# A hybrid recurrent decoder step on one core: weight matrices of the first two feed-forward multiplies begun earlier

## The chip, the core and the metric

The kernel runs on one core of one Trainium2 chip. The metric is the device time of one execution in microseconds (us), the median of several runs; less is better. The engines are called PE (matrix multiply), DVE (vector), ACT (activations), POOL (GpSimd) and SP (the queue that issues the DMA transfers).

## What is computed

One layer over 1032 tokens (1024 of a new sequence and 8 single ones), 1024 wide. The part that the change touches lies between the output projection and the SwiGLU feed-forward:

```python
merged = jnp.concatenate([rmsnorm(lru_out, p['g_lru_out']), rmsnorm(s5_out, p['g_s5_out'])], axis=-1)
x32 = x.astype(F32) + g1 * (merged @ p['w_out'].astype(F32))
hn2 = rmsnorm(x32, p['norm2_g']) * (1.0 + sc2) + sh2
ffn = (jax.nn.silu(hn2 @ p['ffn_w_gate'].astype(F32)) * (hn2 @ p['ffn_w_up'].astype(F32))) @ p['ffn_w_down'].astype(F32)
```

## The kernel before

Every fp32 product is made of three PE products of split operands: a number is held as a high and a low part (`wh`, `wl` of a weight matrix, two planes of a data block), and the kernel multiplies high by high, high by low and low by high. The tokens lie in four quarters of 258; two of them make a half, called z=0 and z=1.

The gate and up multiplies use a recursive scheme with seven products in place of eight (`PRODUCTS`): X A, Z A, X S, Y S, X T, Y T and X D. The first letter is the PSUM bank in which the product gathers, the second the weight matrix: A is loaded as it is, S and T are made of sums and differences of the two loaded pieces, and D is a quarter of the second piece. One product for one half is 12 matmuls of 128x258. `gu_weights(n)` begins matrix n (even numbers are gate matrices, named g0, g1, ...; odd ones up matrices, u0, u1, ...): it issues two loads (`wf_g`, `wf_u`; there are two buffers for all of them), four sums on POOL (`sa`, `sb`) and the split of D. The splits of A, S and T are made when `get` is first called: an ACT copy for the high part and a DVE subtraction for the low one. `roomy` puts T's parts into a big pool of 24 buffers instead of the pool of two for `wh` and `wl`. With `lazy`, which only u0 has, D is split when it is first asked for.

The data of a half become ready in a chain. The output projection adds its units to `xz` on DVE, ACT squares the rows (`sqx`), PE sums the squares over the rows (`pc_n2a` for z=0, `pc_n2b` for z=1), ACT and DVE make the reciprocal root of it, PE spreads it over the partitions (`pb_n`), ACT copies it out (`rb`), and `norm2_steps` multiplies `xz` by it on DVE, scales and shifts on ACT, and splits the result into blocks `b` on ACT and DVE, some of their differences (`vn`) on POOL. The blocks are ready in four groups: B11, B21 (`b1_d_0` for z=1 and each d), T1 and T2 (`b1_d_1`), T3 and T4 (`b1_d_2`).

The stretch between the projection and the regular loop is here called the entry. There g0 and u0 are run for one half at a time, because z=1 isn't ready yet: gate z=0, up z=0, up z=1, then gate z=1 with the gate matrix loaded a second time (g0b). From matrix g1 on both halves are multiplied together. In the entry the order of the instructions of ACT, DVE and POOL is that of the code (`entry` opens a context that says so); PE's order is that of the code throughout, and a scheduler sets SP's. `multiply` runs the functions in `hooks` behind the `after` of a product; `after` copies banks out and hands results to the taker (silu for the gate). The hooks of gate z=0 begin u0 (`u_make`), split g0's S and T, and run the chain above for z=1 (`rstd_b`, `spread_b`, `norm_rest`).

Of the kernel before, what the change touches and what calls it, by code (L numbers as in the profile page):

```python
# [19 lines left out]
T = 1024  # L20
# [34 lines left out]
def body(ctx, tc, a, o):  # L55
    nc = tc.nc
    V, S, G, PE = nc.vector, nc.scalar, nc.gpsimd, nc.tensor
# [13 lines left out]
    def mul(out, x, y, e=None):  # L71
        tt(out, x, y, ALU.mult, e)

    def add(out, x, y, e=None):
        tt(out, x, y, ALU.add, e)

    def sub(out, x, y, e=None):
        tt(out, x, y, ALU.subtract, e)
# [10 lines left out]
    def f(name, w=TX, dt=F32):  # L89
        return fp.tile([P, w], dt, tag="F", name=name, padded_shape=[P, TX])  # L90

    def small(name):
        return psm.tile([P, 512], F32, tag="sm", name=name)

    def split(hi, lo, src, e=None):
        S.activation(hi, src, AF.Copy)
        tt(lo, src, hi.bitcast(F32), ALU.subtract, e)
# [26 lines left out]
    def load_raw(src, name, n=1024):  # L124
        wf = wp.tile([P, n], F32, tag="wf", bufs=2, name=f"wf_{name}")
        nc.sync.dma_start(out=wf, in_=src)
        return wf

    def split_w(wf, name, n=1024, pool=None, tags=("wh", "wl"), e=None):
        q = pool or wp  # L130
        wh = q.tile([P, n], F32R, tag=tags[0], name=f"wh_{name}")
        wl = q.tile([P, n], F32R, tag=tags[1], name=f"wl_{name}")
        split(wh, wl, wf, e)
        return wh, wl
# [14 lines left out]
    def wcols(pair, k):  # L149
        return tuple(t[:, k * P:(k + 1) * P] for t in pair)  # L150

    def acc_bank(name, w=CW):
        return pm.tile([P, 512], F32, tag="mm", name=name)[:, 0:w]
# [529 lines left out]
    after = ExitStack()  # L683
# [389 lines left out]
    for j in range(4, 20):  # L1073
        i = int(R0 + R1 * (j - 4))
# [153 lines left out]
    def four(t):  # L1228
        return t[:, 0:4 * CH].rearrange("p (b n) -> p b n", b=4)
# [6 lines left out]
    def x_load(z):  # L1236
        for d in range(4):
            xz[z].append(four(f(f"xz{z}_{d}", TT)))
            for i in range(2):
                nc.sync.dma_start(out=xz[z][d][:, 2 * i:2 * i + 2], in_=zview(a["xp"][2 * d + i], z))  # L1240
# [119 lines left out]
    def quarter(name):  # L1360
        return chunk(name, CH)
# [105 lines left out]
    TOGETHER = [(i, z) for i in range(7) for z in range(2)]  # L1467
    APART = [(i, z) for z in range(2) for i in range(7)]

    def weights_of(r0, r1, n, name, roomy=False, lazy=False):  # L1470

        sa, sb = (f(f"s{i}_{name}", 2 * n) for i in "ab")
        add(sa[:, 0:n], r1[:, 0:n], r1[:, n:2 * n], G)
        sub(sa[:, n:2 * n], sa[:, 0:n], r0[:, 0:n], G)
        sub(sb[:, 0:n], r0[:, 0:n], r1[:, 0:n], G)
        sub(sb[:, n:2 * n], r0[:, n:2 * n], sa[:, n:2 * n], G)
        src = {"A": r0, "S": sa, "T": sb}
        made = {}

        def make_d():  # L1480
            d = f(f"{name}D", 2 * n, F32R)
            made["D"] = d[:, 0:n], d[:, n:2 * n]
            split(*made["D"], r1[:, n:2 * n])

        if not lazy:
            make_d()

        def get(which, i):
            if which == "D" and lazy and "D" not in made:
                make_d()  # L1490
            if which not in made:
                kw = dict(pool=fp, tags=("F", "F")) if roomy and which == "T" else {}
                made[which] = split_w(src[which], f"{name}{which}", 2 * n, **kw)
            return tuple(t[:, i * n:(i + 1) * n] for t in made[which])

        return get

    def multiply(get, nk, xin, after, order=TOGETHER, hooks={}):

        banks = [{}, {}]  # L1500
        for i, z in order:
            bank, which, half, block = PRODUCTS[i]
            w = get(which, half)
            first = bank not in banks[z]
            if first:
                banks[z][bank] = (small(f"{bank}{z}") if bank == "Z" else acc_bank(f"{bank}{z}", 512))[:, 0:CH]
            b = banks[z][bank]
            for k in range(nk):
                (wh, wl), (xh, xl) = wcols(w, k), xin(z, k)[block]
                PE.matmul(b, lhsT=wh, rhs=xh, start=first and k == 0, stop=False, skip_group_check=True)  # L1510
                PE.matmul(b, lhsT=wh, rhs=xl, start=False, stop=False, skip_group_check=True)  # L1511
                PE.matmul(b, lhsT=wl, rhs=xh, start=False, stop=k == nk - 1, skip_group_check=True)  # L1512
            after(i, z, banks[z])
            for fn in hooks.get((i, z), ()):
                fn()


    NP = NFF // 2

    def gu_weights(n, again=""):  # L1520
        p_, j = divmod(n, 2)
        name = f"{'gu'[j]}{p_}{again}"
        r = [load_raw(a["w_gu"][2 * p_ + i, j], f"{name}_{i}") for i in range(2)]
        return weights_of(*r, 512, name, n in (1, 2 * NP - 1), n == 1)

    def dn_weights(n):

# [24 lines left out]
    def gate_up(u, get, take, **kw):  # L1552
        keep = [{}, {}]

        def after(i, z, b):
            k = keep[z]

            def copy(name, bank):
                k[name] = quarter(f"{name}{z}")
                S.activation(k[name], b[bank], AF.Copy)  # L1560

            if i == 0:
                copy("p1", "X")
            elif i == 1:
                add(k["p1"], b["Z"], k["p1"])
                take(z, 0, k["p1"])
            elif i == 2:
                copy("u2", "X")
            elif i == 3:
                copy("p5", "Y")  # L1570
            elif i == 4:
                copy("u3", "X")
                add(k["u3"], k["u3"], k["p5"], G)
                take(z, 3, k["u3"])
            elif i == 5:
                add(k["u2"], b["Y"], k["u2"])
                take(z, 1, k["u2"])
            else:
                take(z, 2, b["X"])

        multiply(get, 4, lambda z, k: blks[z][k], after, **kw)

    def gate(u):
        return lambda z, at_, src: S.activation(u[z][:, at_], src, AF.Silu)

    def up(u):
        return lambda z, at_, src: mul(u[z][:, at_], src, u[z][:, at_])


    u_first = [four(f(f"u0_{z}", TT)) for z in range(2)]  # L1590
# [11 lines left out]
    for z in range(2):  # L1602
        if z:
            x_load(1)
        for i, (m, c) in enumerate(ordered_units[z]):
            if z or i >= AHEAD:
                half_part(m, c, 0)
            half_part(m, c, 1)
            if z and i == 12:
                g_w = gu_weights(0)  # L1610
                g_w("A", 0)
            if z and i == 14:
                entry.enter_context(tc.manual_schedule(engines={ENG.Activation, ENG.DVE, ENG.Pool}))
            out_add(ubank[m, c], m, c)
            if i % 2:
                out_done(z, i // 2, m)
            if z and i == 0:
                ra = rstd_half(0, "n2a")
            if z and i == 2:
                for _ in norm2_steps(0, spread_half(0, ra)):  # L1620
                    pass

    ONE = [[(i, z) for i in range(7)] for z in range(2)]
# [8 lines left out]
    def go(n):  # L1632
        return lambda: pump(norm_b[1:], n)

    u_w = []

    def u_make():
        u_w.append(gu_weights(1))

    def u_part(which):  # L1640
        return lambda: u_w[0](which, 0)

    def norm_rest():
        entry.close()
        u_part("A")()
        u_part("T")()
        pump(norm_b[1:], 99)

    gate_up(u_first, g_w, gate(u_first), order=ONE[0],
            hooks={(0, 0): [rstd_b, u_make, lambda: g_w("S", 0)], (1, 0): [lambda: g_w("T", 0)],  # L1650
                   (2, 0): [spread_b], (3, 0): [norm_rest]})
    gate_up(u_first, u_w[0], up(u_first), order=ONE[0])
    g_w = gu_weights(0, "b")
    gate_up(u_first, u_w[0], up_first, order=ONE[1])
    gate_up(u_first, g_w, gate_second, order=ONE[1])
    nxt = gu_weights(2)
    kept = []
    for p_ in range(NP):
        if p_ == 0:
            u = u_first  # L1660
        else:
            u = [four(f(f"u{p_}_{z}", TT)) for z in range(2)]
            for j in range(2):
                n = 2 * p_ + j
                get, nxt = nxt, gu_weights(n + 1) if n < 2 * NP - 1 else None
# [62 lines left out]
    for g in range(NG):  # L1728
        nx_blocks = down_blocks(g + 1) if g < NG - 1 else None
        for q in range(4):  # L1730
            n = 4 * g + q
            get, nxt = nxt, dn_weights(n + 1) if n < 4 * NG - 1 else None

            def after(i, z, b):
                row, j, bank = TO[i]
                dst = acc[2 * q + row][:, (z + 2 * j) * CH:(z + 2 * j + 1) * CH]
                add(dst, b[bank], dst)
# [49 lines left out]
    for c, (s, n) in enumerate(LAST):  # L1787
        cc = slice(s, s + n)
        ssc = f(f"ssf{c}", n)
        for m in range(DK):  # L1790
# [13 lines left out]
            if c > 0 and m == SF:  # L1804
                r = rstd_sums(sums, D, f"nf_{c - 1}", LAST[c - 1][1], 2, f)
# [107 lines left out]
```

## Time and profile before

| | us |
|---|---|
| median of 3 runs | 1178.22 (1175.53 to 1181.87) |
| the profiled execution | 1181.37 |
| its span in the profile | 1179.2 |
| PE busy in the span | 1093.7 (93%) |
| DVE busy | 838.2 (71%) |
| ACT busy | 500.9 (42%) |
| POOL busy | 454.7 (39%) |

The profile is of one execution. Its span is what the profiler saw of the core; the time of the same execution is 2.2 us longer. Positions in the span are given as microseconds from its start. The entry lies between about 454 and 523 us.

### The profile page before, as it was taken

What the parts mean: (1) busy time and instruction counts of PE and PEld (TensorE: products, weight loads), DVE (VectorE), ACT (ScalarE), POOL (GpSimd) and SP (SyncE); (2) the same over time, 40 slices, a digit from 0 to 9 for tenths busy, and PEclk for the clock granted to TensorE, in tenths of its full rate; (3) what the DMA queues carried; (4) which work ended last, traced back from release to release, by engine and by line L of the source; (5) the groups of instructions that cost most, each with busy time, mean ns of one, the idle gap of its engine ahead of it and who ended that gap; (6) DMA issues with size and microseconds to landing.
All of it is one profiled execution on the core that took longest, in us unless ns stands there. A gap on an engine that the chain in (4) does not pass through costs nothing.

```text
span 1179.2 us, 21432 instructions
## 1 busy us (share of the span) xinstructions
PE 1093.7 (93%) x8480; PEld 1045.6 (89%) x8480; DVE 838.2 (71%) x1360; ACT 500.9 (42%) x948; POOL 454.7 (39%) x475
## 2 busy tenths in 40 slices
PE   7887888999987999589999999999999999999995
PEld 5776777897967999589999999999999999999995
DVE  6879799854977287765776677677645367778966
ACT  4433323328664155553554454454444531221254
POOL 3396535301030003464654666465532133243022
PEclk8898989899998999799999999999999999999997
DMA  9557445432043302042532443244312967459212
GB/s 339 183 157 214 149 161 156 145 99 73 19 146 108 127 37 81 30 164 100 191 154 93 160 179 145 90 180 180 117 64 75 356 271 289 161 216 298 81 50 95
DMA packets 90627, 174.92 MB, mean 148 GB/s; under 512 B 18720, under 2 KB 54304, under 8 KB 90528
## 3 DMA queue, kind: packets, MB, share of 16 engines
q1 hardware_dynamic: 90528, 173.57, 42.7%
q8 instruction: 66, 1.08, 0.4%
q14 instruction: 33, 0.27, 0.1%
HBM read 126.56 MB, written 46.98 MB: 147 GB/s over the span
## 4 chain that ended last, share of the span: by engine, by line
PE 66%; DVE 10%; ACT 4%; DMA 2%; issue 2%; POOL 1%; DVEq 0%; ACTq 0%; POOLq 0%; SPq 0%
PE X L1510 9%; PE X L1512 9%; PE X L1511 9%; PE Y L1510 4%; PE Y L1512 4%; PE Y L1511 4%; PE o L1309 3%; PE o L1308 3%; PE o L1310 3%; PE Z L1510 2%; PE Z L1511 2%; PE Z L1512 2%; DMA wf_d<-w_dn 1%; DVE acc L69 1%; PE in L144 1%
## 5 line engine op out<-in xcount | busy, mean ns | idle before, releaser
L69 POOL TENSOR_TENSOR u<-u,p 128x258 f32<-128x258 f32 x44 | 40.0, 909 | 130.2 <-ACT u L1560 120.8
L142 PE MATMUL in<-hnh,wh_in 128*128 128x344 f32 (+1 forms) x240 | 82.9, 345 | 0.0
L143 PE MATMUL in<-hnl,wh_in 128*128 128x344 f32 (+1 forms) x240 | 80.1, 334 | 0.0
L144 PE MATMUL in<-hnh,wl_in 128*128 128x344 f32 (+1 forms) x240 | 80.1, 334 | 0.0
L69 POOL TENSOR_TENSOR st_d<-wf_d 128x256 f32<-128x256 f32 x32 | 27.7, 887 | 110.9 <-PE X L1512 37.9
L69 POOL TENSOR_TENSOR sa_g<-wf_g 128x512 f32<-128x512 f32 x11 | 14.2, 1295 | 117.9 <-DVE xz L69 90.4
L69 DVE TENSOR_TENSOR acc<-X,acc 128x258 f32<-128x258 f32 x128 | 49.9, 420 | 10.3 <-PE X L1512 10.1
L142 PEld LDWEIGHTS in<-hnh,wh_in 128*128 128x128 f32 x240 | 48.2, 201 | 2.9 <-issue 2.9
L69 DVE TENSOR_TENSOR hs<-v,hs 128x516 fp32r<-128x516 f32 x32 | 46.3, 1463 | 2.6 <-ACT hs L1380 2.6
L143 PEld LDWEIGHTS in<-hnl,wh_in 128*128 128x128 f32 x240 | 47.9, 200 | 0.0
L144 PEld LDWEIGHTS in<-hnh,wl_in 128*128 128x128 f32 x240 | 47.7, 199 | 0.0
L1560 ACT ACTIVATE u<-X 128x258 f32<-128x258 f32 x88 | 33.1, 381 | 33.8 <-PE X L1512 33.8
L1309 PE MATMUL o<-ls,wh_s 128*128 128x258 f32 x128 | 37.5, 293 | 5.7 <-DVE ls L69 5.7
L87 DVE SCALAR_TENSOR_TENSOR xz<-o,mod,xz 128x258 f32<-128x258 f32 (+1 forms) x32 | 15.2, 481 | 31.4 <-PE o L1310 27.6
L1310 PE MATMUL o<-hs,wl_s 128*128 128x258 f32 x128 | 37.4, 292 | 0.0
L1308 PE MATMUL o<-hs,wh_s 128*128 128x258 f32 x128 | 37.4, 292 | 0.0
L69 POOL TENSOR_TENSOR acc<-acc,rbf 128x388 f32<-128x388 f32 x10 | 11.9, 1218 | 64.7 <-ACT rbf L201 52.9
L1308 PE MATMUL o<-hl,wh_l 128*128 128x258 f32 x128 | 36.6, 286 | 0.0
L1309 PE MATMUL o<-ll,wh_l 128*128 128x258 f32 x128 | 36.5, 285 | 0.0
L1310 PE MATMUL o<-hl,wl_l 128*128 128x258 f32 x128 | 36.1, 282 | 0.0
L69 DVE TENSOR_TENSOR u<-Y,u 128x258 f32<-128x258 f32 x44 | 18.7, 425 | 22.2 <-PE Y L1512 22.1
L69 POOL TENSOR_TENSOR v<-u 128x516 f32<-128x516 f32 x16 | 20.7, 1293 | 34.9 <-DVE u L69 34.9
(1656 smaller groups left out, 4832.2 us busy)
## 6 DMA issues: line engine op xcount, KB each, us to landing
ht<-hs SPq DMA_DIRECT2D x48, 516.0 KB, 3.0
db<-ht SPq DMA_DIRECT2D x48, 516.0 KB, 8.6
ad<-ada SPq DMA_DIRECT2D x48, 512.0 KB, 6.4
wf_g<-w_gu SPq DMA_DIRECT2D x22, 512.0 KB, 3.6
wf_u<-w_gu SPq DMA_DIRECT2D x22, 512.0 KB, 3.4
wf_d<-w_dn SPq DMA_DIRECT2D x16, 512.0 KB, 4.5
wf_in<-w_in SPq DMA_DIRECT2D x10, 512.0 KB, 4.4
x<-xt SPq DMA_DIRECT2D x8, 516.0 KB, 8.0
```

The lines of the kernel that those rows point to most:

```text
L69: (e or V).tensor_tensor(out=out, in0=x, in1=y, op=op)
L87: V.scalar_tensor_tensor(out=out, in0=x, scalar=s, in1=y, op0=op0, op1=op1)
L142: PE.matmul(ps, lhsT=wh, rhs=xh, start=first, stop=False)
L143: PE.matmul(ps, lhsT=wh, rhs=xl, start=False, stop=False)
L144: PE.matmul(ps, lhsT=wl, rhs=xh, start=False, stop=last)
L1308: PE.matmul(b, lhsT=wh, rhs=xh, start=half == 0 and k == 0, stop=False)
L1309: PE.matmul(b, lhsT=wh, rhs=xl, start=False, stop=False)
L1310: PE.matmul(b, lhsT=wl, rhs=xh, start=False, stop=half == 1 and k == 3)
L1510: PE.matmul(b, lhsT=wh, rhs=xh, start=first and k == 0, stop=False, skip_group_check=True)
L1511: PE.matmul(b, lhsT=wh, rhs=xl, start=False, stop=False, skip_group_check=True)
L1512: PE.matmul(b, lhsT=wl, rhs=xh, start=False, stop=k == nk - 1, skip_group_check=True)
L1560: S.activation(k[name], b[bank], AF.Copy)
```

## The change

The gate matrix g0 is begun four units of the projection sooner (unit 8 of z=1 in place of 12), its S and T are split inside the projection (unit 12) and no more in hooks of gate z=0. The up matrix u0 is begun inside the projection (unit 14) and no more in the first hook, its T is split there, and its D is split at once instead of lazily. g0 gets the roomy place for T as well. The spread of the reciprocal root for z=1 is put between the matmuls of product 1 of gate z=0 and the `after` of that product, by a new kind of hook (`pre`), in place of the hook of product 2. A and S of u0 are split in the hooks of products 1 and 2.

```diff
-    def multiply(get, nk, xin, after, order=TOGETHER, hooks={}):
+    def multiply(get, nk, xin, after, order=TOGETHER, hooks={}, pre={}):
...
+            for fn in pre.get((i, z), ()):
+                fn()
             after(i, z, banks[z])
...
-        return weights_of(*r, 512, name, n in (1, 2 * NP - 1), n == 1)
+        return weights_of(*r, 512, name, n in (0, 1, 2 * NP - 1))
...
-            if z and i == 12:
+            if z and i == 8:
                 g_w = gu_weights(0)
                 g_w("A", 0)
+            if z and i == 12:
+                g_w("S", 0)
+                g_w("T", 0)
             if z and i == 14:
+                u_w = gu_weights(1)
+                u_w("T", 0)
                 entry.enter_context(tc.manual_schedule(engines={ENG.Activation, ENG.DVE, ENG.Pool}))
...
-    u_w = []
-
-    def u_make():
-        u_w.append(gu_weights(1))
-
-    def u_part(which):
-        return lambda: u_w[0](which, 0)
+    def part(get, which):
+        return lambda: get(which, 0)
 
     def norm_rest():
         entry.close()
-        u_part("A")()
-        u_part("T")()
         pump(norm_b[1:], 99)
 
     gate_up(u_first, g_w, gate(u_first), order=ONE[0],
-            hooks={(0, 0): [rstd_b, u_make, lambda: g_w("S", 0)], (1, 0): [lambda: g_w("T", 0)],
-                   (2, 0): [spread_b], (3, 0): [norm_rest]})
-    gate_up(u_first, u_w[0], up(u_first), order=ONE[0])
+            pre={(1, 0): [spread_b]},
+            hooks={(0, 0): [rstd_b], (1, 0): [part(u_w, "A")], (2, 0): [part(u_w, "S")], (3, 0): [norm_rest]})
+    gate_up(u_first, u_w, up(u_first), order=ONE[0])
     g_w = gu_weights(0, "b")
-    gate_up(u_first, u_w[0], up_first, order=ONE[1])
+    gate_up(u_first, u_w, up_first, order=ONE[1])
```

The order of the instructions is set by the code and the scheduler together, so three places of it are shown, before and after.

On ACT, from the split of g0's D to the two copies `rb` of the spread, the order before is this (`sqx_2` are the squares of the last rows of z=1, `p_4700` and `u_4767` copies of banks, `u_0` the silu):

```order
L96 ACTIVATE g0D<-wf_g_1_4581 128x512
L1322 ACTIVATE sqx_2_4626<-xz_2_4099 128x516 x2
L1560 ACTIVATE p_4700<-X_4687 128x258
L1400 ACTIVATE pc_n2b<-pc_n2b,epst 128x129
L96 ACTIVATE wh_g0S<-sa_g_4583 128x1024
L1584 ACT_TABLE_LOAD
L1584 ACTIVATE u_0_3738<-p_4700 128x258
L96 ACTIVATE wh_g0T<-sb_g_4584 128x1024
L96 ACTIVATE wh_u0T<-sb_u_4727 128x1024
L1560 ACTIVATE u_4767<-X_4687 128x258
L1413 ACTIVATE rb_0_4772<-pb_n_4769 128x258
L1413 ACTIVATE rb_1_4777<-pb_n_4774 128x258
```

And after the change the same stretch of ACT is this:

```order
L96 ACTIVATE g0D<-wf_g_1_4467 128x512
L1325 ACTIVATE sqx_1_4567<-xz_1_4096 128x1032
L96 ACTIVATE wh_g0S<-sa_g_4469 128x1024
L96 ACTIVATE wh_g0T<-sb_g_4470 128x1024
L1322 ACTIVATE sqx_2_4634<-xz_2_4099 128x516
L96 ACTIVATE u0D<-wf_u_1_4663 128x512
L1322 ACTIVATE sqx_2_4634<-xz_2_4099 128x516
L1562 ACTIVATE p_4725<-X_4712 128x258
L1400 ACTIVATE pc_n2b<-pc_n2b,epst 128x129
L96 ACTIVATE wh_u0T<-sb_u_4666 128x1024
L1413 ACTIVATE rb_0_4763<-pb_n_4760 128x258
L1413 ACTIVATE rb_1_4768<-pb_n_4765 128x258
```

The splits of g0's S and T and of u0's D have moved ahead of the last squares; the `rb` copies now stand ahead of the table load and the silu, but still behind `wh_u0T`, which reads the POOL sum `sb_u`.

On DVE, around the last rows of `xz` of z=1 and the first multiply by `rb`, the order before is this:

```order
L87 SCALAR_TENSOR_TENSOR xz_2_4099<-o_1_4628,mod,xz_2_4099 128x258
L87 SCALAR_TENSOR_TENSOR xz_2_4099<-o_3_4656,mod,xz_2_4099 128x250
L69 TENSOR_TENSOR go_3_4682<-o_3_4656,mod 128x8
L69 TENSOR_TENSOR xz_2_4099<-go_3_4682,xz_2_4099 128x8
L1402 RECIPROCAL r_n2b<-pc_n2b 128x129
L69 TENSOR_TENSOR wl_g0S<-sa_g_4583,wh_g0S 128x1024
L69 TENSOR_TENSOR p_4700<-Z_4736,p_4700 128x258
L69 TENSOR_TENSOR wl_g0T<-sb_g_4584,wh_g0T 128x1024
L69 TENSOR_TENSOR wl_u0T<-sb_u_4727,wh_u0T 128x1024
L69 TENSOR_TENSOR xz_0_4093<-xz_0_4093,rb_0_4772 128x2x258
```

And after the change the same place on DVE is this:

```order
L87 SCALAR_TENSOR_TENSOR xz_2_4099<-o_1_4636,mod,xz_2_4099 128x258
L69 TENSOR_TENSOR u0D<-wf_u_1_4663,u0D 128x512
L87 SCALAR_TENSOR_TENSOR xz_2_4099<-o_3_4681,mod,xz_2_4099 128x250
L69 TENSOR_TENSOR go_3_4707<-o_3_4681,mod 128x8
L69 TENSOR_TENSOR xz_2_4099<-go_3_4707,xz_2_4099 128x8
L1402 RECIPROCAL r_n2b<-pc_n2b 128x129
L69 TENSOR_TENSOR p_4725<-Z_4747,p_4725 128x258
L69 TENSOR_TENSOR wl_u0T<-sb_u_4666,wh_u0T 128x1024
L69 TENSOR_TENSOR xz_0_4093<-xz_0_4093,rb_0_4763 128x2x258
```

The low part of u0's D, which came behind all blocks of z=1, now stands ahead of the last rows of `xz`; the low parts of g0's S and T are gone from between the reciprocal and the first multiply.

On SP, the queue of loads around u0 and g0b, as a difference (`xd` writes finished rows of `xz` back to memory):

```order
 L1331 DMA xd_0_3476<-xz_0_4093 128x1032
 L1331 DMA xd_1_3477<-xz_1_4096 128x1032
-L126 DMA wf_u_0_4722<-w_gu 128x1024
-L126 DMA wf_u_1_4724<-w_gu 128x1024
+L126 DMA wf_u_0_4661<-w_gu 128x1024
+L126 DMA wf_u_1_4663<-w_gu 128x1024
+L126 DMA wf_g0b_5041<-w_gu 128x1024
 L1331 DMA xd_2_3478<-xz_2_4099 128x1032
-L126 DMA wf_g0b_5041<-w_gu 128x1024
 L126 DMA wf_g0b_5043<-w_gu 128x1024
```

The loads themselves keep their order; only the first load of g0b has passed one write. Its buffer is that of u0's second piece, which is free once u0's D and the POOL sums have been made.

## Rows read from the trace of the kernel before

**Rows 1.** By stretch: us; busy PE, PEld, DVE, ACT, POOL; PEclk; DMA share, GB/s

```profile
454.00:523.00 69.00, 50.39 (x378) 48.05 (x377) 48.82 (x73) 39.22 (x74) 32.25 (x25) 0.85 0.24 77
...
600.00:900.00 300.00, 300.00 (x2506) 300.00 (x2505) 210.28 (x233) 143.03 (x289) 166.91 (x125) 1.00 0.37 134
```

**Rows 2.** PE's waits from 400 to 523: total, times, longest

```profile
PE X L1510 <- ACT u0D L96: 7.8, 1, 7.8
PE Y L1510 <- ACT p L1560: 5.1, 2, 3.4
PE X L1512 <- DVE u0D L69: 3.0, 1, 3.0
PE X L1512 <- DVE wl_g0S L69: 1.7, 1, 1.7
PE X L1512 <- DVE wl_g0bT L69: 0.5, 1, 0.5
```

**Rows 3.** PE's longest wait behind the entry, from 523 on

```profile
PE pc_nf L181 <- DVE ssf L69: 3.6, 2, 2.4
```

**Rows 4.** PE in the entry: start, duration, instruction, idle time before it

```profile
457.94 0.36 PE L1510 MATMUL X<-b,wh_g0S 128*128 128x258 f32 x1
...
462.30 1.76 PE L1410 MATMUL pb_n<-r_n2b,ident 128*128 128x129 f32 x8
463.81 0.37 PE L1510 MATMUL Y<-b,wh_g0S 128*128 128x258 f32 x1
...
489.40 0.58 PE L1510 MATMUL X<-b,u0D 128*128 128x258 f32 x1 [7.82 <-ACT u0D L96]
...
498.03 0.28 PE L1510 MATMUL Z<-b,wh_u0A 128*128 128x258 f32 x1
...
518.43 0.58 PE L1510 MATMUL Y<-b,wh_g0bT 128*128 128x258 f32 x1 [3.44 <-ACT p L1560]
...
522.89 0.28 PE L1510 MATMUL X<-b,wh_g1A 128*128 128x258 f32 x1
```

**Rows 5.** A stretch behind the longest wait, columns as in rows 1

```profile
494.00:498.00 4.00, 4.00 (x21) 4.00 (x20) 1.32 (x2) 0.63 (x1) 1.49 (x2) 0.51 0.39 131
```

**Rows 6.** DVE around and in the entry

```profile
438.73 0.42 DVE L69 TENSOR_TENSOR vn<-xz,vn 128x258 f32<-128x258 f32 x1
...
440.15 1.32 DVE L69 TENSOR_TENSOR vn<-xz,vn 128x258 f32<-128x258 f32 x1
...
448.13 1.22 DVE L69 TENSOR_TENSOR sqx<-sqx,sqx 128x1032 f32<-128x1032 f32 x1
...
454.07 0.48 DVE L87 SCALAR_TENSOR_TENSOR xz<-o,mod,xz 128x250 f32<-128x250 f32 x1 [2.39 <-PE o L1310]
...
465.47 2.51 DVE L69 TENSOR_TENSOR xz<-xz,rb 128x516 f32<-128x516 f32 x4
...
487.90 1.89 DVE L69 TENSOR_TENSOR b<-vn,b 128x516 fp32r<-128x516 f32 x3
...
492.48 0.68 DVE L69 TENSOR_TENSOR u0D<-wf_u,u0D 128x512 fp32r<-128x512 f32 x1
```

**Rows 7.** ACT: the split of u0's T and the copies of the spread

```profile
463.06 1.04 ACT L96 ACTIVATE wh_u0T<-sb_u 128x1024 fp32r<-128x1024 f32 x1
...
464.28 0.65 ACT L1413 ACTIVATE rb<-pb_n 128x258 f32<-128x258 f32 x2
```

**Rows 8.** POOL: a sum of g0, and the first and last of u0's four sums

```profile
439.89 1.30 POOL L69 TENSOR_TENSOR sa_g<-wf_g 128x512 f32<-128x512 f32 x1 [90.36 <-DVE xz L69]
...
455.11 1.28 POOL L69 TENSOR_TENSOR sa_u<-wf_u 128x512 f32<-128x512 f32 x1 [8.47 <-DMA wf_u<-w_gu]
...
458.95 2.27 POOL L69 TENSOR_TENSOR sb_u<-wf_u,sa_u 128x512 f32<-128x512 f32 x1
```

**Rows 9.** SP's issue of u0's two loads

```profile
450.01 0.81 SPq L126 DMA_DIRECT2D wf_u<-w_gu  x2
```

**Rows 10.** The load with the longest median landing among the page's DMA issues

```profile
db<-ht SPq DMA_DIRECT2D x48, 516.0 KB, 8.6
```

## The prediction, made before the change was run

> **What bounds the kernel now.** I read the busy times by stretch first, then PE's waits, then the places of the waits on PE's timeline, and last the engines that PE waits for. In the regular loop PE is the bound: 300.00 of 300 us busy, 2506 matmuls, so 0.12 us for one and 12 x 0.12 = 1.44 us for a product of one half [rows 1]. In the entry it is not: 50.39 of 69.00 us busy, at a mean clock of 0.85 [rows 1]. PE's waits there name whom it waits for: ACT and DVE with u0's D (7.8 and 3.0 us), ACT with a bank copy (5.1 us, two times), DVE with the low part of g0's S (1.7) and of g0b's T (0.5) [rows 2]. Behind the entry no wait is above 3.6 us, and that one is the final norm's [rows 3]. So a change of the entry is worth what it takes from the entry, provided that nothing that it delays stands in the loop.
>
> DVE is the entry's second load: 48.82 us busy of 69 [rows 1]. Its longest chain runs from the first multiply by `rb` at 465.47 to the end of the third group of blocks (T1, T2 of z=1) at 487.90 + 1.89 = 489.79, 24.3 us [rows 6]. When PE's own waits go, this chain is what PE meets next; the whole forecast turns on it.
>
> **What the change removes.** (a) g0's S is split inside the projection, so PE doesn't wait for it. From its first matmul at 457.94 to the first of the next product at 463.81 there are 5.87 us [rows 4]. The product is worth 1.44; the spread `pb_n` in between took 1.51, of which a lower clock may have made half, so it is worth 0.75 to 1.51. Lost: 2.9 to 3.7 us; I take 3.6, as PE had just stood still. (b) u0's D is split early: waits of 7.8 and 3.0 us [rows 2]. PE then runs at a granted clock of 0.51, the lower of its two levels (1.2 GHz) [rows 5]: from 489.40 to 498.03 it has two products' work, 8.63 - 3.0 - 2 x 1.44 = 2.75 us over [rows 4]. Together 13.6. (c) The first of the two waits for a bank copy, 5.1 - 3.4 = 1.7 [rows 2]: its copy stands behind scalings on ACT, and some of those stay ahead of it. I expect it to stay in kind. (d) The waits for g0b's T and for the copy in front of its last products, 0.5 + 3.4 [rows 2], and the clock behind: from 518.43 to 522.89 are 4.46 us for two products of 1.44, 1.6 over [rows 4]. Together 5.5. Gross, (a) to (d): 24.4 us. That would be the gain if nothing were late next.
>
> **What is late next.** First the start of DVE's chain. u0's loads were issued at 450.01 [rows 9], as soon as DVE's g0D had been made, which now stands ahead of an add of 1.22 us and a row update of about 0.48 (their durations in [rows 6]): 1.6 sooner, 448.4. The load landed when POOL began to sum, 455.11 - 450.01 = 5.1 later [rows 8, 9]: now 453.5. The four sums took 455.11 to 458.95 + 2.27 = 461.2, 6.1 us [rows 8]: now to 459.6. `wh_u0T` (1.04) on ACT waits for the last one, and the two `rb` copies (0.65 for the pair) stand behind it [rows 7]. So `rb` comes at about 461, whatever the spread does: the earlier place of the spread on PE is not what sets it. On DVE `wl_u0T` stands ahead of the multiply (1.2 us, by the add of 1.22 with two inputs of about the same size [rows 6]): 459.6 + 1.04 + 1.22 = 461.9. The chain begins 3.6 us sooner than at 465.47. Below, if the sums run at 1.28 each [rows 8], it is a further 1.0; I leave that out.
>
> u0D on DVE (0.68 [rows 6]) now stands ahead of the last rows of `xz`. Load at 453.5, about 0.6 for ACT's half-size copy (by 1.04 for the full size [rows 7]) and 0.68: those rows start at 454.8, where they started at 454.07 [rows 6]. PE's row sums and the spread are 0.7 late, which the wait of `rb` for POOL's sums covers: squares, row sums, root, reciprocal and spread have until 460.6. That cover goes if the landing is late, and then sums and rows are late together.
>
> With the chain's own 24.3 us the third group ends at 486.2. Everything in the chain (the low parts of u0's A and S, the differences, the splits) is still in it. What is new in it is POOL. g0b's second load stood behind u0's D on DVE, which was made at 492.48 [rows 6], when the blocks were done; so its four sums came when DVE had little to do. Now that load waits only for u0's A, and the four sums run beside DVE's last groups of blocks. What that costs is seen where g0's sums ran beside the first half's norm: a difference of 128x258 took 1.32 us at 440.15, beside a POOL sum that began at 439.89 and took 1.30 [rows 6, 8], and 0.42 at 438.73 without one [rows 6]. So one sum can cost DVE 0.9 us, and up to 1.3 if the instruction waits for the whole of it: four cost 0 (they find gaps) to 5.2. I take 4.4, nearer the upper end, because DVE's splits there follow one another without a gap (three in the row at 487.90). The third group ends at 490.6; bounds 486.2 and 491.4.
>
> This agrees with a rule of the Trainium skill, "SBUF — State Buffer", section "Who interferes with whom", which speaks against this change: a DVE instruction with two inputs in SBUF and a GpSimd instruction that reads SBUF exclude each other on a shared port, and the later one fully blocks. By the rule the four sums cost about their upper bound; if it did not hold here they would cost nothing. The row at 440.15 agrees with it: 1.32 us in place of 0.42.
>
> PE, without waits, gets to the third group's product early. From about 459.3 (row sums at 456, 1.0 for them, product Z, the spread) it has five products of gate z=0, seven of up z=0 and two of up z=1: 14 x 1.44 = 20.2, and the 1.6 of (c): 481, and some 482 by the matmuls that need this group's last block. So it waits 4 to 9 us there, mostly for DVE's blocks, some of it a product earlier. From the end of the group PE has 0.36 (three matmuls) and eleven products, 15.8, to the first product of g1: 490.6 + 16.2 = 506.8. To that I add the lower clock behind the wait, 1.5 (between 0 and the 2.75 of (b)), and 2.0 for what remains of (d): its copy isn't queued behind the same transfer any more, but other copies still are; bounds 0 and 5.5. Sum: 510.3, where it was 522.89. **The gain is 12.6 us.** Ends: 486.2 + 16.2 = 502.4, a gain of 20.5; and 491.4 + 16.2 + 2.75 + 5.5 = 515.9, a gain of 7.0.
>
> Behind the entry the order of all engines is the same, and g1's loads come with PE's products of g0b, so I put nothing there.
>
> The profiled execution took 1181.37 us (its span 1179.2, and 2.2 around it): 1181.4 - 12.6 = 1168.8. The median of the runs is 1178.22, 3.15 less, so 1165.6: I predict 1166.
>
> **Rivals.** *The sums cost nothing.* For it: sums and blocks may interleave, and some of DVE's instructions there read PSUM. Against it: 440.15. Then 502.4 and 0 to 2 of the tail: a gain of 18.5 to 20.5, so 1158 to 1160. *DVE and POOL take nearly all.* The sums hit the chain in full, the wait for the copy (d) stays, and the splits of g0b come late too, since DVE makes them behind the blocks: the 7.0 shrinks by a wait of the size of the present one for the copy, 3.4, to 3.6; 1171 to 1176. Against it: g0b's second load no longer waits for the end of the blocks, so its splits have slack. *Slower.* u0D's load is late. DVE stands still in front of the last rows of `xz`, and row sums, root, `rb` and all of z=1 with them; POOL's sums are as late. Each us of landing behind 453.5 takes a us from the gain; at 466 it is gone, and it decides for slower by over 0.5% from about 472. The page's longest median landing is 8.6 us [rows 10], 3.5 more than assumed: 1169. So only an outlier does this; the time would be above 1184. *It doesn't do what it says.* The spread is ahead of the silu, but `rb` still waits for `wh_u0T`; that is in the sum. Should `wl_g0S` or u0D yet be waited for, 3.6 or up to 13.6 return, and the time is 1169 to 1178.
>
> **Chances.** Forecast with colliding sums 0.62; sums free 0.20; nearly all taken 0.10; not what it says 0.05; slower 0.03. The range takes the bounds (1158 to 1171) and most of the third case: 1158.5 to 1174. A measurement of this kernel can tell about 0.5%, 5.9 us, from no change, so faster means below 1172.3: all of the first two cases and a part of the others, 0.85; same 0.11; slower 0.04.
>
> **What would show it.** Right: PE has no wait for `wl_g0S` and none for u0D; the first multiply by `rb` starts near 462; PE's longest wait in the entry is 4 to 9 us, for DVE's blocks `b` of z=1, in up z=1; POOL's g0b sums lie at 480 to 490, and DVE's splits of `vn` beside them last over a us; g1's first product at about 510. Wrong: PE's row sums `pc_n2b` after 458 (the load was late); DVE's splits at their usual length beside the sums (a gain near 20); a wait for `p` or for g0b's parts of over 4 us in gate z=1; waits in the loop behind g1.

## The result: 1.26% faster, and the profile after

The changed kernel takes 1164.73 us (median of 4 runs, 1164.02 to 1168.10); the kernel before, on the same chip, 1178.39. The ratio is 0.9874, 95% interval 0.9855 to 0.9893. The forecast was 1166, range 1158.5 to 1174. The profiled execution took 1164.80 us, its span is 1162.8.

First PE's waits from 400 to 523 in the changed kernel (total, times, longest; compare [rows 2]):

```profile
PE X L1511 <- DVE b L69: 3.1, 3, 1.1
PE X L1510 <- ACT u L1562: 2.8, 4, 1.3
PE pc_n2b L1396 <- ACT sqx L1322: 1.3, 1, 1.3
PE X L1510 <- ACT p L1562: 0.4, 1, 0.4
```

No wait for u0's D is left, none for g0's S and none for g0b's T. The largest sum is for DVE's blocks `b`, as forecast, in three pieces of 1.0 to 1.1 us. By stretch, with the columns of [rows 1]:

```profile
454.00:509.00 55.00, 47.25 (x377) 44.69 (x377) 48.06 (x68) 35.10 (x69) 32.68 (x25) 0.94 0.20 63
...
490.00:494.00 4.00, 4.00 (x18) 4.00 (x19) 4.00 (x8) 1.64 (x3) 0.00 (x0) 0.50 0.02 4
...
509.00:586.00 77.00, 77.00 (x645) 77.00 (x644) 54.48 (x60) 37.43 (x79) 44.28 (x34) 1.00 0.46 162
```

PE and POOL have as many instructions in the entry as in [rows 1], give or take one; ACT and DVE have five fewer each, among them the splits of g0's S and T. The entry is 55 us long instead of 69: what went is mostly standing still. DVE is now busy for 48.06 of 55.00 us. Behind the wait for the blocks PE is granted 0.50, its lower level of 1.2 GHz, for some us; behind the entry there is no gap. PE's timeline at the places of [rows 4] (start, duration, instruction, idle time before it):

```profile
453.95 0.28 PE L1510 MATMUL X<-b,wh_g0A 128*128 128x258 f32 x1
...
457.68 0.43 PE L1396 MATMUL pc_n2b<-sqx,ones 128*32 128x129 f32 x8 [1.34 <-ACT sqx L1322]
459.58 1.39 PE L1410 MATMUL pb_n<-r_n2b,ident 128*128 128x129 f32 x8
...
484.41 0.39 PE L1510 MATMUL X<-b,wh_u0S 128*128 128x258 f32 x1 [0.43 <-ACT p L1562]
...
490.00 0.58 PE L1511 MATMUL X<-b,wh_u0S 128*128 128x258 f32 x1 [1.02 <-DVE b L69]
...
490.60 0.42 PE L1510 MATMUL Y<-b,wh_u0S 128*128 128x258 f32 x1
...
493.18 0.42 PE L1510 MATMUL X<-b,wh_u0T 128*128 128x258 f32 x1
...
509.05 0.28 PE L1510 MATMUL X<-b,wh_g1A 128*128 128x258 f32 x1
```

g1's first product starts at 509.05, where it was 522.89 [rows 4]: 13.8 us sooner. The medians differ by 13.7, so the entry accounts for the gain. The two profiled executions differ by 16.6; the rest of that lies behind the entry, 1.5 us of it in the down multiply.

DVE's chain (compare [rows 6]):

```profile
454.58 1.22 DVE L69 TENSOR_TENSOR u0D<-wf_u,u0D 128x512 fp32r<-128x512 f32 x1 [1.00 <-ACT u0D L96]
...
460.65 1.23 DVE L69 TENSOR_TENSOR wl_u0T<-sb_u,wh_u0T 128x1024 fp32r<-128x1024 f32 x1 [0.45 <-ACT wh_u0T L96]
461.80 3.72 DVE L69 TENSOR_TENSOR xz<-xz,rb 128x516 f32<-128x516 f32 x6
...
482.76 3.48 DVE L69 TENSOR_TENSOR b<-vn,b 128x516 fp32r<-128x516 f32 x2
...
486.50 1.43 DVE L69 TENSOR_TENSOR b<-vn,b 128x516 fp32r<-128x516 f32 x1
...
487.85 1.50 DVE L69 TENSOR_TENSOR u<-u,u 128x258 f32<-128x258 f32 x1
```

and POOL's sums for g0b, beside the last three of these rows:

```profile
482.63 1.35 POOL L69 TENSOR_TENSOR sa_g0b<-wf_g0b 128x512 f32<-128x512 f32 x1 [2.31 <-DVE b L69]
483.95 1.74 POOL L69 TENSOR_TENSOR sb_g0b<-wf_g0b,wf_g0b 128x512 f32<-128x512 f32 x1
...
487.45 1.61 POOL L69 TENSOR_TENSOR sb_g0b<-wf_g0b,sa_g0b 128x512 f32<-128x512 f32 x1
```

The first multiply by `rb` starts at 461.80 (465.47 before [rows 6]). Three splits of `vn` in a row took 1.89 us before [rows 6]; now two take 3.48, and a product of 128x258, 0.41 before, takes 1.50. PE's last wait for the third group ends at 490.00.

The landing of g0b's load is not what set the start of these sums: its second load was issued at 466.73 and took at most 4.0 us. The sums stand behind POOL's own differences `vn` and an addition, which end at 480.3, and then wait 2.31 us for a block of DVE.

### The profile page after: what moved, and what is told of

It is laid out like the page before. It is cut to its first block, busy times and chain, and to the rows that moved or that the text cites. A ratio compares the mean times of both kernels' runs of the same rounds, so it can differ in the third digit from the quotient of the medians.

```text
span 1162.8 us, 21429 instructions
## 1 busy us (share of the span) xinstructions
PE 1088.8 (94%) x8480; PEld 1042.0 (90%) x8480; DVE 843.9 (73%) x1360; ACT 499.8 (43%) x948; POOL 456.3 (39%) x475
## 4 chain that ended last, share of the span: by engine, by line
PE 70%; DVE 17%; ACT 5%; issue 4%; POOL 2%; DMA 1%; SPq 0%; DVEq 0%; ACTq 0%; POOLq 0%
PE X L1510 9%; PE X L1511 9%; PE X L1512 9%; PE Y L1510 5%; PE Y L1511 5%; PE Y L1512 5%; PE o L1308 2%; PE o L1309 2%; PE o L1310 2%; PE Z L1511 2%; PE Z L1512 2%; PE Z L1510 2%; DVE rw L69 1%; PE in L142 1%; PE in L143 1%
## 5 line engine op out<-in xcount | busy, mean ns | idle before, releaser
L69 DVE TENSOR_TENSOR acc<-Y,acc 128x258 f32<-128x258 f32 x64 | 26.7, 424 | 10.4 <-PE Y L1512 9.5
```

Source lines behind the costliest of these rows:

```text
L69: (e or V).tensor_tensor(out=out, in0=x, in1=y, op=op)
```

## The experiments

Theory: the waits for u0's D were the largest loss, and what is left is set by DVE's chain of blocks, from the first multiply by `rb` to the third group, stretched by POOL's sums. Main rivals: the early start of both matrices makes the gain by itself; every wait of PE counts by itself; POOL's sums cost nothing; the spread ahead of the silu is the heart of it.

The table gives for each kernel the ratio of its time to the kernel before on the same chip, and from its trace three times counted from PE's first matmul of g0: the first multiply by `rb` on DVE (chain), PE's first matmul of Y S in up z=1, for which X S must be done (Y S), and PE's first matmul of g1 (entry). The kernel before took 1180 to 1181 us there (median), so ratios are compared and not times.

| kernel | ratio (95%) | chain | Y S | entry |
|---|---|---|---|---|
| before | 1 | 11.60 | 47.05 | 69.02 |
| changed | 0.9874 (0.9855 to 0.9893) | 7.85 | 36.65 | 55.10 |
| changed, again | 0.9874 (0.9858 to 0.9890) | 7.88 | 36.66 | 55.09 |
| u0's D lazy again | 0.9924 (0.9906 to 0.9942) | 7.23 | 42.75 | 61.11 |
| before with u0's D at once | 0.9968 (0.9954 to 0.9982) | 12.15 | 41.37 | 63.11 |
| g0 late again | 0.9918 (0.9897 to 0.9940) | 9.45 | 43.08 | 60.24 |
| spread late again | 0.9872 (0.9853 to 0.9890) | 10.50 | 37.51 | 55.39 |
| g0's sums kept | 0.9835 (0.9814 to 0.9856) | 7.95 | 32.49 | 51.40 |
| g0's sums kept, again | 0.9819 (0.9801 to 0.9836) | 7.95 | 32.45 | 50.52 |
| constants for sums | 0.9838 (0.9820 to 0.9857) | 7.77 | 32.31 | 50.96 |
| sums kept, T and D behind rb | 0.9855 (0.9834 to 0.9875) | 5.71 | 32.69 | 52.50 |
| two products more, early | 0.9903 (0.9880 to 0.9926) | 7.84 | 40.00 | 57.47 |
| two products more, in up z=1 | 0.9908 (0.9892 to 0.9925) | 7.78 | 36.35 | 58.86 |
| sums kept, two products more | 0.9847 (0.9828 to 0.9865) | 7.85 | 34.14 | 52.50 |

**The changed kernel again**, unedited:

> The changed kernel once more, unedited, beside the following ones on the same chip. 0.9855 to 0.9893 of the kernel before again, its entry 55.1 us from g0's first product to g1's.

Ratio 0.9874 and an entry of 55.09 us: both come back.

**u0's D lazy again, the rest of the change kept.**

```diff
-        return weights_of(*r, 512, name, n in (0, 1, 2 * NP - 1))
+        return weights_of(*r, 512, name, n in (0, 1, 2 * NP - 1), n == 1)
```

> The changed kernel with one part undone: u0's D is split lazily again, behind all blocks of z=1. Theory (the wait for u0's D was the main loss, and DVE's chain of blocks decides what is left): PE stands again in front of u0's D, from about 479 to the end of the last group of blocks plus the split, about 489; then 15 products of 1.44 and the low clock behind the wait: g1's first product near 517, some 8 us later than in the changed kernel, time 1171 to 1175. POOL's sums for g0b then lie behind the blocks again. Rival (the early start of the chain and of g0's S is the main part): under 4 us lost, 1168 or less.

The entry is 6.0 us longer than in the changed kernel, the ratio 0.5% worse. The waits come back (PE's waits, 440 to 523):

```profile
PE X L1510 <- ACT u0D L96: 5.2, 1, 5.2
PE X L1512 <- DVE u0D L69: 4.0, 1, 4.0
```

That is below the 8 us of the theory and above the rival's 4. PE's 9.2 us of waits for u0's D come in place of the 3.5 for the blocks and the copy in front of them: POOL's sums leave the blocks alone here (they start 4 us behind the last block), and PE waits for no block.

**u0's D at once, alone, in the kernel before.**

```diff
-        return weights_of(*r, 512, name, n in (1, 2 * NP - 1), n == 1)
+        return weights_of(*r, 512, name, n in (1, 2 * NP - 1))
```

> The kernel before with one part of the change alone: u0's D is split at once instead of lazily, nothing is begun earlier. Theory: PE's waits for u0's D (7.8 and 3.0 us) are replaced by a wait for the third group of blocks, which ends near 489.8 plus up to 4 us for POOL's sums that now run beside it; g1's first product near 513 to 515, so 8 to 10 us of the 13.8 are already there: time 1168.5 to 1171. Rival (the early begin of both matrices makes the gain, as the moved lines suggest): under 4 us, 1174.5 or more.

The entry is 5.9 us shorter than before in the trace; the ratio says 0.32%, 3.8 us, with an interval of 2.1 to 5.4 us. The profiled execution, of 1173.7 us, was among the fastest of ten (1173.5 to 1179.1). The theory's 8 to 10 was wrong; by the ratio the rival's "under 4" holds, though not beyond the interval. PE's waits, 440 to 523, show what came instead:

```profile
PE X L1511 <- DVE b L69: 4.0, 5, 1.7
PE X L1512 <- DVE wl_g0bT L69: 2.9, 1, 2.9
```

The chain starts 0.55 later than before, as u0's D stands ahead of it on DVE, and POOL's sums run into the blocks. So u0's D alone makes a quarter (by the ratios) to two fifths (by the traces) of the gain; the rest comes with the other parts of the change.

**g0 begun at unit 12 again, its S and T in hooks again.**

```diff
-            if z and i == 8:
+            if z and i == 12:
                 g_w = gu_weights(0)
                 g_w("A", 0)
-            if z and i == 12:
-                g_w("S", 0)
-                g_w("T", 0)
...
-            hooks={(0, 0): [rstd_b], (1, 0): [part(u_w, "A")], (2, 0): [part(u_w, "S")], (3, 0): [norm_rest]})
+            hooks={(0, 0): [rstd_b, part(g_w, "S")], (1, 0): [part(g_w, "T"), part(u_w, "A")], (2, 0): [part(u_w, "S")], (3, 0): [norm_rest]})
```

> The changed kernel with g0 begun at unit 12 as before, its S and T split in hooks of gate z=0 as before; u0 is still begun at unit 14, its D split at once, and the spread early. Theory (DVE's chain is the bound, started by rb behind POOL's sums of u0): u0's load is issued near 450 again, so the first multiply by rb comes near 464 in place of 461.8, and g0's T (1.2 us) stands inside the chain: 3 to 3.5 us later at the end, time 1167.5 to 1168.5. PE's wait for g0's S comes back, but PE only waits less for the blocks later on. Rival (each wait of PE counts by itself): 3.6 for g0's S on top, 7 us, 1171.5 or more.

5.1 us longer: between theory and rival. PE's waits for `pc_n2b` and for bank copies, and ACT in front of the second copy:

```profile
457.00 0.43 PE L1396 MATMUL pc_n2b<-sqx,ones 128*32 128x129 f32 x8 [2.60 <-ACT sqx L1322]
...
478.09 0.39 PE L1510 MATMUL X<-b,wh_u0S 128*128 128x258 f32 x1 [2.55 <-ACT p L1562]
...
492.38 0.54 PE L1510 MATMUL X<-b,wh_u0S 128*128 128x258 f32 x1 [2.19 <-ACT p L1562]
```

```profile
491.42 0.63 ACT L96 ACTIVATE g0bD<-wf_g0b 128x512 fp32r<-128x512 f32 x1 [6.58 <-DVE b L69]
491.95 0.37 ACT L1562 ACTIVATE p<-X 128x258 f32<-128x258 f32 x1
```

u0's load is 1.2 us later, and so are the row sums (a wait of 2.60 where it was 1.34): the lateness of the load goes through one to one, as the rival "slower" of the prediction had it. The chain starts 1.6 later. PE's wait for g0's S, which theory and rival both expected back, does not come: the spread now stands on PE between product Z A and X S. The rest of the 5.1 us is new: PE waits for several bank copies, the largest waits 2.55 and 2.19, and at the second of these the scheduler put g0b's D ahead of the copy on ACT; it waits 6.58 us for DVE, and PE waits for the copy behind it.

**The spread behind product 2 again.**

```diff
-            pre={(1, 0): [spread_b]},
-            hooks={(0, 0): [rstd_b], (1, 0): [part(u_w, "A")], (2, 0): [part(u_w, "S")], (3, 0): [norm_rest]})
+            hooks={(0, 0): [rstd_b], (1, 0): [part(u_w, "A")], (2, 0): [spread_b, part(u_w, "S")], (3, 0): [norm_rest]})
```

> The changed kernel with only the spread undone: it stands in the hook of product 2 again, behind the silu and its table load on ACT. Theory (rb is held by POOL's sums of u0 and the split of u0's T behind them, so the earlier spread is worth only what ACT puts ahead of rb): rb comes some 3 us later, but DVE splits u0's A (1.2 us) while it waits, so the chain of blocks ends 1.5 to 2 us later: 0.13 to 0.17% slower than the changed kernel. Rival (the spread ahead of the silu is the heart of the change): 5 us or more lost, 0.4% or more.

The chain starts 2.65 later, DVE splits u0's A meanwhile, and the entry is 0.3 us longer; the ratio doesn't differ. That is less than the theory's 1.5 to 2, and the rival falls: the new place of the spread is worth nothing that can be measured here.

**g0's sums kept for g0b, no sums made a second time.**

```diff
-        sa, sb = (f(f"s{i}_{name}", 2 * n) for i in "ab")
-        add(sa[:, 0:n], r1[:, 0:n], r1[:, n:2 * n], G)
...
+        if sums:
+            sa, sb = sums
+        else:
+            sa, sb = (f(f"s{i}_{name}", 2 * n) for i in "ab")
+            add(sa[:, 0:n], r1[:, 0:n], r1[:, n:2 * n], G)
...
-    g_w = gu_weights(0, "b")
+    g_w = gu_weights(0, "b", g_w.sums)
```

> The changed kernel, but g0b doesn't make its four POOL sums a second time: the sums of g0 are kept in their buffers and split again. Theory (the sums stretch DVE's splits beside them by about 4 us, and the chain of blocks sets the end of the entry): DVE's splits of vn in the last groups last 0.6 to 0.7 us each instead of 1.4 to 1.8, the third group ends near 486, PE's wait in up z=1 is shorter by 4, g1's first product at 504 to 505.5, time 1160 to 1161. Rival (sums find gaps, the chain is set by ACT's copies or PE): under 1 us, 1164 or more.

The third group of blocks on DVE in this kernel:

```profile
480.43 1.29 DVE L69 TENSOR_TENSOR b<-vn,b 128x516 fp32r<-128x516 f32 x2
...
481.98 0.68 DVE L69 TENSOR_TENSOR b<-vn,b 128x516 fp32r<-128x516 f32 x1
...
482.92 1.29 DVE L69 TENSOR_TENSOR b<-vn,b 128x516 fp32r<-128x516 f32 x2
```

A split takes 0.65 again. The chain runs from 459.46 to 482.92 + 0.65 = 483.6, 24.1 us, where the changed kernel's ran from 461.80 to about 490.0, 28.2: the sums cost 4.1. The entry is 3.7 us shorter. Once more, beside the changed kernel on one chip:

> The kernel with the kept sums once more, unedited, beside the changed kernel on the same chip: 3.5 to 4.6 us faster than it (0.30 to 0.39%), its entry near 51.2 us.

The entry is 4.6 us shorter, and the ratio 0.9819 against 0.9874: this version beats both. By the medians it is 7.0 us faster, more than expected. In the two profiled executions, also 7 us apart, the other 2.6 lie ahead of the entry, where the edit changes nothing: g0's first product comes at 451.61 in place of 454.22.

**POOL kept busy without reading.** g0b's S and T are constants here, so that part of the computation is left out.

```diff
+        if name == "g0b":
+            for t in (sa, sb):
+                for j in range(4):
+                    G.memset(t, float(j))
+        else:
-        add(sa[:, 0:n], r1[:, 0:n], r1[:, n:2 * n], G)
+            add(sa[:, 0:n], r1[:, 0:n], r1[:, n:2 * n], G)
...
```

> The changed kernel, but in place of g0b's four POOL sums POOL fills the same two buffers with constants, eight times 128x1024, which keeps it busy at the same place for some 7.6 us, and reads nothing from SBUF (g0b's S and T are constants, so that part of the computation is left out). Theory (a DVE operation with two SBUF inputs is held up by POOL's reading, not by POOL being busy): DVE's splits of vn beside it last 0.6 to 0.7 us, as with the kept sums, and the entry is 3.5 to 4.5 us shorter than in the changed kernel. Rival (any POOL work on SBUF beside DVE holds it up): the splits last 1.4 us or more, and the entry is as long as in the changed kernel.

POOL and, below, DVE at the same time:

```profile
482.36 0.97 POOL L1476 MEMSET sa_g0b<- 128x1024 f32 x1 [2.28 <-issue]
483.25 0.96 POOL L1476 MEMSET sb_g0b<- 128x1024 f32 x1
484.14 0.97 POOL L1476 MEMSET sa_g0b<- 128x1024 f32 x1
```

```profile
482.51 1.29 DVE L69 TENSOR_TENSOR b<-vn,b 128x516 fp32r<-128x516 f32 x2
...
484.05 0.68 DVE L69 TENSOR_TENSOR b<-vn,b 128x516 fp32r<-128x516 f32 x1
```

POOL writes without a break, DVE's splits keep their 0.65 us, and the entry is 4.1 us shorter than in the changed kernel. The rival falls: POOL's sums, which read, hold DVE up; POOL being busy with writing does not.

**Sums kept, and u0's T and D split behind the rb copies.** The lines that keep the sums are those shown above and are left out here.

```diff
-        return weights_of(*r, 512, name, n in (0, 1, 2 * NP - 1))
+        return weights_of(*r, 512, name, n in (0, 1, 2 * NP - 1), n == 1, sums)
...
                 u_w = gu_weights(1)
-                u_w("T", 0)
...
-            hooks={(0, 0): [rstd_b], (1, 0): [part(u_w, "A")], (2, 0): [part(u_w, "S")], (3, 0): [norm_rest]})
+            hooks={(0, 0): [rstd_b], (1, 0): [part(u_w, "A")], (2, 0): [part(u_w, "S"), part(u_w, "D")], (3, 0): [part(u_w, "T"), norm_rest]})
```

> The changed kernel with g0's sums kept for g0b (no POOL sums beside the blocks), and u0's T and D split behind the rb copies instead of ahead of them. Theory: row sums no more wait for u0's D (1.3 us), rb comes right behind the spread, and the first multiply starts 1.9 us sooner; but the two splits (1.2 and 0.7 us) now stand inside the chain, so it ends 0 to 0.5 sooner than with the kept sums alone: the entry 0 to 0.5 us shorter than with the kept sums alone, time the same to its measurement, 1160 to 1162 on the chip of those runs. Rival (the begin of the chain decides, whatever stands inside it): 2 us shorter than with the kept sums alone.

The chain starts 2.2 sooner, near the 1.9 expected, and PE doesn't wait for blocks at all, as it doesn't with the kept sums alone; yet the entry is 1.1 to 2.0 us longer than there. PE waits 3.3 us for two copies of the Y bank on ACT:

```profile
490.64 0.39 PE L1514 MATMUL Y<-b,wh_u0T 128*128 128x258 f32 x1 [1.86 <-ACT p L1566]
...
502.42 0.39 PE L1514 MATMUL Y<-b,wh_g0bT 128*128 128x258 f32 x1 [1.46 <-ACT p L1566]
```

Both theories miss: the chain is no longer the bound there.

**Two products more on PE**, between gate z=0 and up z=0 of the changed kernel:

```diff
+    idle = small("idle")[:, 0:CH]
+    for r in range(2):
+        for k in range(4):
+            (wh, wl), (xh, xl) = wcols(g_w("D", 0), k), blks[0][k]["T4"]
+            PE.matmul(idle, lhsT=wh, rhs=xh, start=r == 0 and k == 0, stop=False, skip_group_check=True)
...
     gate_up(u_first, u_w, up(u_first), order=ONE[0])
```

> The changed kernel with two products more on PE (24 matmuls of 128x258, a repeat of g0's last product into a bank that nobody reads) between gate z=0 and up z=0, 2.9 us of PE work. Theory (DVE's chain of blocks is the bound until the third group of blocks is done): PE only waits less in up z=1, g1's first product comes 0 to 0.8 us later, maybe sooner by up to 1, as the shorter wait keeps the clock up. Rival (PE's own work decides, and its waits are a few tenths here and there): 2.9 us later, 0.25% slower than the changed kernel.

2.4 us longer, near the rival. But the scheduler had again put g0b's D ahead of a bank copy on ACT, and PE waited 3.2 us for that copy (ACT, then PE):

```profile
488.90 0.63 ACT L96 ACTIVATE g0bD<-wf_g0b 128x512 fp32r<-128x512 f32 x1 [5.35 <-DVE b L69]
489.44 0.37 ACT L1562 ACTIVATE p<-X 128x258 f32<-128x258 f32 x1
```

```profile
489.86 0.58 PE L1510 MATMUL X<-b,wh_u0S 128*128 128x258 f32 x1 [3.22 <-ACT p L1562]
```

So it was done again, in up z=1 behind Z A (a hook of product 1, with u0's D in place of g0's), where ACT, DVE and POOL keep their order up to this place:

> The changed kernel with two products more on PE (24 matmuls, 2.9 us, a repeat of u0's last product into a bank that nobody reads), now in up z=1 itself, between its products Z A and X S, where PE waits for the third group of blocks; up to there ACT, DVE and POOL keep their order, which the earlier place of these products did not. Theory (DVE's chain is the bound up to the third group): the entry is 0 to 0.5 us longer than in the changed kernel, or up to 1 shorter, as PE stands still for less and its clock stays up. Rival (PE's work counts in full): 2.9 us longer.

3.8 us longer, worse than the rival. PE's timeline says where:

```profile
487.91 0.39 PE L1511 MATMUL X<-b,wh_u0S 128*128 128x258 f32 x1 [1.39 <-DVE b L69]
...
493.02 0.58 PE L1510 MATMUL X<-b,wh_u0T 128*128 128x258 f32 x1 [2.50 <-ACT u L1562]
```

and ACT between the two:

```profile
488.50 0.64 ACT L96 ACTIVATE g0bD<-wf_g0b 128x512 fp32r<-128x512 f32 x1 [5.29 <-DVE b L69]
491.33 0.42 ACT L1595 ACTIVATE u<-p 128x258 f32<-128x258 f32 x1 [2.19 <-DVE p L69]
491.65 1.04 ACT L96 ACTIVATE wh_g0bT<-sb_g0b 128x1024 fp32r<-128x1024 f32 x1
492.60 0.37 ACT L1562 ACTIVATE u<-X 128x258 f32<-128x258 f32 x1
```

Up to the third group the theory holds: Y S starts at 36.35, 0.3 sooner than in the changed kernel, though PE did 2.9 us more. Behind it ACT waits for DVE with another copy, and that copy and a split stand ahead of the copy that PE needs. PE waits 2.50 us for it, and runs at its lower clock until about 499, where that lasted until 494 in the changed kernel. The same products with the sums kept:

> The same two products in the same place, but in the kernel that keeps g0's sums for g0b. Theory (without POOL's sums the chain ends near the time at which PE comes, so PE's own work is the bound again): 2.2 to 2.9 us longer than with the kept sums alone, near the length of the changed kernel's entry less 1.5. Rival (DVE still the bound): under 1 us longer.

There Y S comes 1.7 later and the entry is 1.1 to 2.0 longer: PE's work counts, in part taken up by the 0.5 to 0.9 that PE waited for a copy at that place. The theory holds in kind, and the rival falls; by the entry the size is below the 2.2 to 2.9 expected. By the medians on the same chip it is 3.4 us, with four executions of each spread over 4 us.

## Why the prediction was right

**Removed waits.** (a), (b) and the first part of (d) are gone, (c) stayed in kind with 1.3. Of (d) 0.7 us is left (a bank copy in front of g0b's last product), where 2.0 was put.

**Start of the chain.** Forecast 461.9, measured 461.80. The prediction said that the place of the spread doesn't set it, and putting the spread back cost 0.3 us. The trace shows the path that it named. POOL's last sum, then ACT's split of u0's T:

```profile
458.24 1.29 POOL L69 TENSOR_TENSOR sb_u<-wf_u,sa_u 128x512 f32<-128x512 f32 x1
```

```profile
459.56 1.06 ACT L96 ACTIVATE wh_u0T<-sb_u 128x1024 fp32r<-128x1024 f32 x1 [1.05 <-POOL sb_u L69]
```

On DVE `wl_u0T` follows at 460.65 and the multiply behind it; the `rb` copies are done at 461.4. The spread is not far off: it begins at 459.58, and the `rb` copies at 460.53.

**Length of the chain.** Forecast 24.3 and 4.4 for the sums; 24.1 (with the sums kept) and 4.1 measured. That the 24.3 came back is in part luck. In the kernel before it held 2.14 us of waiting for ACT, which the prediction carried over as if it were work:

```profile
477.74 1.02 DVE L69 TENSOR_TENSOR b<-xz,b 128x516 fp32r<-128x516 f32 x1 [2.14 <-ACT b L1380]
```

In the kernel with kept sums DVE waits 0.65 us in the chain and works 23.4 instead of 22.2:

```profile
459.46 3.72 DVE L69 TENSOR_TENSOR xz<-xz,rb 128x516 f32<-128x516 f32 x6
...
469.57 0.43 DVE L69 TENSOR_TENSOR p<-Z,p 128x258 f32<-128x258 f32 x1 [0.65 <-ACT xz L1431]
```

The Trainium skill, "SBUF — State Buffer", section "Who interferes with whom", says that a DVE instruction with two SBUF inputs contends with a GpSimd instruction that reads SBUF, and not with one that only writes it. The traces agree on both: 0.65 us for a split alone and beside constants, 1.4 to 1.7 beside sums. The rival in which the sums cost nothing put the gain at 18.5 to 20.5 us; the kernels that keep the sums have an entry 17.6 to 18.5 shorter than before.

**PE's wait for the blocks.** Forecast 4 to 9 us; it was 3.1, and 0.4 for a copy in front, below the range. PE began X S of up z=1 at 484.41 instead of 481. Of these 3.3 us, 1.4 were there when gate z=0 reached X S (460.72 instead of 459.3): the row sums waited 1.34 for the last rows, as u0's D took 1.22 on DVE beside a POOL sum instead of 0.68. Waits for bank copies took 2.6 instead of 1.6, and the products somewhat more than 1.44 each. It cost next to nothing, as the chain was the bound: 2.9 us more of PE's work at that place did not make Y S later.

**Behind it.** 16.2 us of products and 1.5 for the clock from 490.6; from 490.00 it was 19.05 in all, of which the two products behind the wait took 2.58 and 1.95 us for 1.44 each, 1.65 over. The sum was 510.3, the trace says 509.05. The tail of (d) was 1.3 shorter than put; the 0.6 by which the chain ended sooner is cancelled by some 0.5 in the rest of the products.

**The parts.** Undone alone, u0's early D is worth 6.0 us of the entry, the early g0 5.1 and the spread 0.3, of 13.9 in all. These don't add up to shares: without the early g0 the scheduler's order on ACT changed too, and u0's D alone made 3.8 to 5.9. No run takes u0's earlier start alone, nor the roomy place of g0's T; what each is worth is not shown. And 3.7 to 4.6 us of the entry were given back by the change itself, by the sums that it moved beside the blocks.

## What to carry to other kernels

When a wait on a late weight is taken away, look for the next engine whose chain starts at a fixed point, and time that chain alone: its start, its length and the price of the collision gave the end of the entry within 1.3 us, though some terms cancelled. Look whether the chain's length holds waits that won't come back. Ask where the freed transfers put their follow-up work: a load that comes sooner lets its sums run sooner, here beside the busiest stretch of another engine; keeping the sums that were already made took a further 3.7 to 4.6 us from the entry. And read ACT's order again behind each edit where a scheduler sets it: an instruction that waits for DVE, ahead of a bank copy that PE waits for, cost 2 to 3 us in three of these kernels.

## What was not expected

Two products added inside a wait of PE made the entry 3.8 us longer, though the wait itself took them up (Y S 0.3 sooner): all of the loss came behind it, from the order on ACT, with a new wait of 2.50, and from PE's lower clock, which lasted some 5 us longer. POOL can write 128x1024 constants one after the other, 0.97 us each, beside DVE's splits without any cost to them.
